# Hybrid encoder trunk on one core: HT as eight tiles that also hold the first adaLN weights, a division moved behind the weighted sums, gelu moved to where its results are loaded

## Chip, cores and metric

One core of one Trainium2 chip runs the whole kernel. The metric is the device time of one execution in microseconds (us), as the median of several runs. "Profile" means one execution taken by the hardware profiler. TensorE is named PE in its rows (PEld its weight loads), VectorE DVE, ScalarE ACT, GpSimd POOL, SyncE SP.

## What is computed

A two-layer encoder trunk on x of 1024 frames x 1024 channels, float32 in and out. Each layer runs a mixer and a feed-forward part, each behind an RMS norm with adaLN shift and scale and a gated residual:

```python
for layer in range(DEPTH):
    mod = cond @ ada_w[layer] + ada_b[layer]
    sh1, sc1, g1, sh2, sc2, g2 = jnp.split(mod, 6, axis=-1)
    h = modulate(rms_norm(x, ln_mix_g[layer]), sh1, sc1)
    ...
    x = x + g1[:, None, :] * mix
    h = modulate(rms_norm(x, ln_ffn_g[layer]), sh2, sc2)
    x = x + g2[:, None, :] * swiglu(h, ffn_w_in[layer], ffn_w_out[layer])
```

Layer 0 mixes with chunked softmax attention (8 heads of 64, clipped relative bias) beside an S5 scan, whose output goes through gelu and a gate; layer 1 with retention (4 heads of 128) beside stick-breaking attention. The two places of layer 0 that the change touches:

```python
p = jax.nn.softmax(s, axis=-1).astype(vb.dtype)
return jnp.einsum('bhqk,bkhd->bqhd', p, vb)
...
y = jax.nn.gelu(y.reshape(bsz, L, B_WIDTH))
gate = jax.nn.sigmoid(y @ w_glu.astype(f32) + b_glu.astype(f32))
return (y * gate).astype(u.dtype)
```

## The kernel before

**Dense products.** Every dense product keeps float32 accuracy by splitting each operand into a high part (rounded to fp32r) and a low part (the rest); `mm3` (L235) issues three matmuls, hi x hi, hi x lo, lo x hi, so rows of lines L237, L238 and L239 come in threes. The normed activations, transposed, are `HT` (L173): one tile of 128 partitions x 2 (hi, lo) x 8 (k) x 1024 frames. Streamed weights come through four `raw` buffers, and `Stream.split` (L125) makes hi and lo in one of six `whl` slots (128 x 2 x 1024) or, for the feed-forward output weights, of two `wo` slots: ScalarE copies hi (L130), GpSimd subtracts for lo (L131). The hidden activations of the feed-forward parts are `aT` (128 x 2 x 1024 each). A row mm<-HT,whl is a matmul into a bank "mm" whose streaming operand (named first) is a slice of HT or of whl, whichever the source code passes second; a row at<-aT,wo is the feed-forward output product.

**Where they lie.** In the built program, HT starts at byte 2,176 of each partition (hi of k at 2,176 + 4,096 k, lo 32,768 further on), whl slot j at 85,216 + 8,192 j, the aT tiles at 186,208 + 8,192 j, and the wo slots at 210,784 and 218,976. lo follows hi by 4,096 bytes in whl, wo and aT.

**Banks.** PSUM has three "mm" banks (L224), four "at" banks (L227) and one "av" bank (L230).

**Order.** The program is written as generators on a clock of ticks (`Pipe`, L42): `yield n` puts the rest of a step n ticks later, and each tick also pumps the weight stream. A feed-forward tick issues 24 large products. The tile layer then places the instructions on each engine; inside `high_priority` they go as early as they may.

**The opening** (`first`, L345). Eight x tiles are loaded and squared, `rms` (L303) turns the sums into 1/rms per frame: column sums on TensorE (L309), a power on GpSimd, a diagonal tile on VectorE (L319), and a product with ones that spreads it over the partitions (L325). The adaLN shift and scale of each k come from `cols(k)`: eight 32-row products of the silu'd condition with the ada0 weights (L370, into the av bank), a copy on ScalarE (L373), two one-column products (L376), and two additions on VectorE (L379, L381). ada0 weights pass through three rooms: two in U (a tile needed only later) and one of their own; the load of k + 3 is issued when k is done (L382). `scale(k)` multiplies x by 1/rms (L389), `turn(k)` applies shift and scale and writes hi (L396) and lo (L397) of HT's row k, and the first projection (wu) follows k by k in five banks. `s5_params` (L723) computes the scan's parameters in many VectorE steps of 16 elements; its first call stands behind n == 0 (L430).

**Attention** (`a_unit`, L581, 64 units: 8 heads x 8 tiles of queries). Scores on TensorE, bias and row minimum on VectorE (L590), Exp with row sums on ScalarE (L595), the reciprocal of the sums and a multiply of the 128 x (128 to 640) weights on VectorE (L597, L598), transposes (L503) and their copies, and products with v into the av bank; after four units of a head pair, hi is copied (L615) and lo subtracted (L616) into HT.

**Scan and gate.** `s5_block` (L916) ends each of its eight blocks with gelu out of PSUM on ScalarE (L974), then transposes (L985) and writes to DRAM; `glu` (L993) loads that twice, once through the weight stream (`yglu`, which gets hi and lo) and once as `yv`, for the last multiply. Rows ACT_TABLE_LOAD are ScalarE's loads of a function table; here they stand at L974 and at L595 (Exp).

**Norms behind a residual.** `norm` (L328) calls `rms` for 512 frames, then writes HT's rows through two "nf" buffers. Behind the first feed-forward part, four `v_tile` steps (L451) project v, and their copies `ve` (L460) out of PSUM also use "nf".

## Time and profile before

| | |
|---|---|
| Three runs | 2706.62, 2700.36, 2694.06 us; median 2700.36 us |
| Profiled execution | own time 2702.07 us, span of its records 2700.3 us |
| Mean granted TensorE clock | 0.982 |
| Instructions | 32542 |
| Busy: TensorE, its weight loads | 2591.9 us (96% of the span), 2115.7 us |
| Busy: VectorE, ScalarE, GpSimd | 1161.8, 709.3, 812.5 us |
| Moved by DMA | 267.11 MB |

The time of a run covers the span and a little around it (1.8 us in the profiled execution). TensorE's matmuls overlap: the next one starts before the last has ended, so "busy" is time in which at least one is under way, and the pace is read from start to start. The granted clock is a fraction of full speed, 2.4 GHz.

### The profile page before, as it was taken

The page shows a single profiled execution, that of the slowest core. Times are in us where ns is not written, and L with a number is a line of the kernel's source. Part 1 is how long each engine was busy: PE and PEld are TensorE (multiplying, and loading weights), DVE is VectorE, ACT ScalarE, POOL GpSimd, SP SyncE. Part 2 cuts the span into 40 slices and gives each one's busy share as a digit, 9 for nine tenths or more (in the row PEclk, how much of TensorE's full clock was granted, in tenths as well). Part 3 has the DMA queues.
Part 4 walks back from the last instruction along what each step waited for, and adds up shares of the span by engine and source line. Part 5 has one row for each costly group of instructions (what it writes and reads, how often), then busy time and mean ns, then how long its engine had stood idle before and what let it go on. Part 6 is the DMA issues. An engine that isn't in the chain of part 4 may idle for free. (4 is left out here: it accounts for less than half of the span.)

```text
span 2700.3 us, 32542 instructions
## 1 busy us (share of the span) xinstructions
PE 2591.9 (96%) x12880; PEld 2115.7 (78%) x12880; DVE 1161.8 (43%) x2164; ACT 709.3 (26%) x1287; POOL 812.5 (30%) x536
## 2 busy tenths in 40 slices
PE   5999898999999999999999999999999999999999
PEld 3898676777888888888778778787778888888887
DVE  7376675464333322222521466765632222222223
ACT  4332567322111111111221344444321111111100
POOL 4365103423322222222212133333232222222211
PEclk8999999999999999999999999999999999999999
DMA  7277764543233311111234332234311111111101
GB/s 274 82 227 226 191 188 150 180 140 109 86 110 109 109 48 47 47 47 47 78 94 152 91 100 86 62 95 152 109 63 47 47 47 47 47 47 47 48 16 63
DMA packets 145479, 267.11 MB, mean 99 GB/s; under 512 B 34416, under 2 KB 82224, under 8 KB 144560
## 3 DMA queue, kind: packets, MB, share of 16 engines
q1 hardware_dynamic: 145328, 265.05, 31.0%
q8 instruction: 101, 1.65, 0.3%
q14 instruction: 50, 0.41, 0.1%
HBM read 221.22 MB, written 45.88 MB: 99 GB/s over the span
## 5 line engine op out<-in xcount | busy, mean ns | idle before, releaser
L238 PE MATMUL mm<-HT,whl 128*128 128x512 f32 x1744 | 694.8, 399 | 2.6 <-DVE HT L340 2.5
L239 PE MATMUL mm<-HT,whl 128*128 128x512 f32 x1744 | 693.9, 398 | 0.0
L237 PE MATMUL mm<-HT,whl 128*128 128x512 f32 x1744 | 691.9, 398 | 0.2
L131 POOL TENSOR_TENSOR whl<-raw,whl 128x1024 fp32r<-128x1024 f32 x142 | 346.3, 2447 | 670.6 <-ACT whl L130 665.0
L238 PEld LDWEIGHTS mm<-HT,whl 128*128 128x128 f32 x1744 | 329.9, 189 | 85.0 <-DVE HT L340 5.1
L237 PEld LDWEIGHTS mm<-HT,whl 128*128 128x128 f32 x1744 | 329.5, 189 | 81.0 <-ACT HT L624 0.7
L239 PEld LDWEIGHTS mm<-HT,whl 128*128 128x128 f32 x1744 | 329.7, 189 | 80.0 <-issue 1.0
L1323 DVE SCALAR_TENSOR_TENSOR x<-at,col,x 128x512 f32<-128x512 f32 x352 | 262.7, 750 | 270.7 <-PE at L239 270.5
L1308 DVE TENSOR_TENSOR sg<-sg,mm 128x512 f32<-128x512 f32 x88 | 60.5, 688 | 666.2 <-PE mm L239 666.1
L239 PE MATMUL at<-aT,wo 128*128 128x512 f32 x704 | 275.5, 391 | 0.0
L237 PE MATMUL at<-aT,wo 128*128 128x512 f32 x704 | 275.4, 394 | 0.0
L238 PE MATMUL at<-aT,wo 128*128 128x512 f32 x704 | 275.3, 391 | 0.0
L237 PE MATMUL mm<-whl,HT 128*128 128x512 f32 (+1 forms) x688 | 252.3, 367 | 9.1 <-ACT ve L460 5.9
L238 PE MATMUL mm<-whl,HT 128*128 128x512 f32 (+1 forms) x688 | 248.2, 361 | 0.0
L239 PE MATMUL mm<-whl,HT 128*128 128x512 f32 (+1 forms) x688 | 245.7, 362 | 0.0
L131 POOL TENSOR_TENSOR wo<-raw,wo 128x1024 fp32r<-128x1024 f32 x44 | 105.4, 2416 | 442.6 <-ACT wo L130 442.5
L130 ACT CAST whl<-raw 128x1024 fp32r<-128x1024 f32 x154 | 161.0, 1053 | 193.0 <-PE mm L239 178.3
L1310 POOL TENSOR_TENSOR aT<-sg,aT 128x512 fp32r<-128x512 f32 x88 | 116.3, 1322 | 306.2 <-DVE aT L1309 298.3
L1307 ACT ACTIVATE sg<-mm 128x512 f32<-128x512 f32 x88 | 52.5, 597 | 540.8 <-PE mm L239 540.8
L130 ACT CAST wo<-raw 128x1024 fp32r<-128x1024 f32 x44 | 44.1, 1047 | 497.3 <-PE at L239 490.1
L237 PEld LDWEIGHTS mm<-whl,HT 128*128 128x128 f32 x688 | 138.6, 201 | 27.7 <-ACT ve L460 6.7
L237 PEld LDWEIGHTS at<-aT,wo 128*128 128x128 f32 x704 | 132.6, 188 | 29.8 <-issue 0.5
(290 smaller groups left out, 3221.7 us busy)
## 6 DMA issues: line engine op xcount, KB each, us to landing
raw<-in_ffn_w_in SPq DMA_DIRECT2D x88, 512.0 KB, 3.5
raw<-in_ada_w SPq DMA_DIRECT2D x80, 512.0 KB, 4.1
raw<-in_ffn_w_out SPq DMA_DIRECT2D x44, 512.0 KB, 3.3
qkd<-stk SPq DMA_DIRECT2D x32, 256.0 KB, 4.7
q<-qkd SPq DMA_DIRECT2D x64, 128.0 KB, 4.1
ks<-qkd SPq DMA_DIRECT2D x32, 256.0 KB, 4.4
qkd<-stk SPq DMA_DIRECT2D x16, 512.0 KB, 2.8
raw<-in_cd_w_in_c SPq DMA_DIRECT2D x16, 512.0 KB, 4.4
```

Of the source, the lines that this page charges most:

```text
L130: nc.scalar.copy(hi, u.raw[:, :u.n])
L131: self.low.tensor_sub(lo, u.raw[:, :u.n], hi.bitcast(F32))
L237: mm(out, lhs.hi, rhs.hi, start=start, stop=False)
L238: mm(out, lhs.hi, rhs.lo, start=False, stop=False)
L239: mm(out, lhs.lo, rhs.hi, start=False, stop=stop)
L1307: nc.scalar.activation(sg, gu[0], AF.Silu)
L1308: nc.vector.tensor_mul(sg, sg, gu[1])
L1310: nc.gpsimd.tensor_sub(a[m].lo[:, sl], sg, a[m].hi[:, sl].bitcast(F32))
L1323: nc.vector.scalar_tensor_tensor(xh, ps, self.col[layer, 5][:, n:n + 1], xh, M, A)
```

## The change

It has these parts:

1. **HT** becomes eight tiles, one for each k, of 128 x 2 x 1024, so that lo of a k follows hi by 4,096 bytes (`Rows` picks the tile). In the built program they start at 2,272 + 8,192 k; whl starts at 85,216 as before; aT at 186,272 and wo at 210,848.
2. **Opening.** The ada0 weights of k are loaded into the room of HT's tile k, all issued ahead, with one load of the weight stream behind every second k, so no load waits for a room. The columns of k + 1 and the products of k + 2 are started ahead of the first projection's products of k - 1, the low parts of streamed weights are made by VectorE instead of GpSimd in this stage, multiplies by 1/rms move into `turn`, and `params` is not called behind n == 0.
3. **Attention.** Reciprocal and multiply of the weights go (L597, L598). Row sums of four units of a head pair are collected in `rc` (128 x 4 x 2); behind the last, one reciprocal, a broadcast to 128 x 512 on GpSimd, four transposes into an "at" bank, a copy on ScalarE and a multiply with the av bank on VectorE, and then hi and lo.
4. **Gelu** leaves the scan's blocks: ScalarE copies there, and gelu runs on the streamed `yglu` tiles ahead of their split (4 of 1024 columns) and on `yv` (2 of 2048) in the gate.
5. **Norms.** `rms` waits two ticks instead of one between the sums and the diagonal tile, and `v_tile` behind the first feed-forward part takes its copies from the "hf" buffers instead of "nf".

The core of the diff (`PAD` was 0 and goes; the order of three small constants in the constructor changes too):

```diff
@@ Stream.split
+        if u.act is not None:
+            nc.scalar.activation(u.raw[:, :u.n], u.raw[:, :u.n], u.act)
         nc.scalar.copy(hi, u.raw[:, :u.n])
@@ Trunk.__init__
-        HT = self.const.tile([P, 2, NK, T], F32R, name="HT")
-        self.HT = Split(HT[:, 0], HT[:, 1])
+        self.ht = [self.const.tile([P, 2, T], F32, tag=f"HT{k}", name="ada0") for k in range(NK)]
+        self.HT = Split(Rows(self.ht, 0), Rows(self.ht, 1))
@@ rms
-        yield 1
+        yield 2
@@ first
+        ada0 = list(self.ht)
+
         def load(k):
             for q in range(2):
-                c0 = q * 1024
-                nc.sync.dma_start(out=slot(k)[:, c0:c0 + 1024], in_=I["ada0"][k, :, q * 1024:(q + 1) * 1024])
+                nc.sync.dma_start(out=ada0[k][:, q], in_=I["ada0"][k, :, q * 1024:(q + 1) * 1024])
...
-            if k + 3 < NK:
-                load(k + 3)
             yield
-        def scale(k):
+        def turn(k):
+            self.ht[k] = self.const.tile([P, 2, T], F32R, tag=f"HT{k}", name="HT")
             for half in range(2):
                 sl = slice(half * 512, half * 512 + 512)
                 v.tensor_mul(xs[:, k, sl], xs[:, k, sl], self.rb[half])
...
-        load(0)
-        self.stream.dma()
-        load(1)
-        load(2)
-        self.stream.dma()
+        for k in range(NK):
+            load(k)
+            if k % 2:
+                self.stream.dma()
...
+        self.stream.low = v
+        live = [cols(k) for k in range(NK)]
...
             if n < NK:
-                next(live[n])
-                scale(n)
                 turn(n)
                 if n + 1 < NK:
-                    live.append(cols(n + 1))
-                    next(live[-1])
-            if n == 0:
-                next(params)
+                    next(live[n + 1])
+                if n + 2 < NK:
+                    next(live[n + 2])
...
+        self.stream.low = nc.gpsimd
@@ a_unit
-        nc.scalar.activation(pw[:, :W], pw[:, :W], AF.Exp, bias=st[:, 0:1], scale=-1.0, accum_out=st[:, 2:3])
-        yield 1
-        nc.vector.reciprocal(st[:, 3:4], st[:, 2:3])
-        nc.vector.tensor_scalar(pw[:, :W], pw[:, :W], st[:, 3:4], None, M)
-        yield 1
+        if i % 4 == 0 and hd % 2 == 0:
+            self.rc = self.sm.tile([P, 4, 2], F32, tag="arc", bufs=2, name="arc")
+        rc = self.rc
+        nc.scalar.activation(pw[:, :W], pw[:, :W], AF.Exp, bias=st[:, 0:1], scale=-1.0, accum_out=rc[:, i % 4, hd % 2:hd % 2 + 1])
+        yield 2
...
+        if i % 4 == 3:
+            nc.vector.reciprocal(rc, rc)
+            f = pool.tile([P, 640], F32, tag="pw", bufs=5, name="af")[:, :512]
+            nc.gpsimd.tensor_copy(f.rearrange("p (a d) -> p a d", d=64),
+                                  rc.rearrange("p i u -> p (i u)").unsqueeze(2).to_broadcast([P, 8, 64]))
...
+        rb = self.at_bank()
+        for j in range(4):
+            nc.tensor.transpose(rb[:, j * P:j * P + P], f[:, j * P:j * P + P], self.ident)
...
-        nc.scalar.copy(hi, av)
-        nc.vector.tensor_sub(lo, av, hi.bitcast(F32))
+        nc.scalar.copy(f, rb)
+        nc.vector.tensor_mul(f, f, av)
+        nc.scalar.copy(hi, f)
+        nc.vector.tensor_sub(lo, f, hi.bitcast(F32))
@@ s5_block
-        nc.scalar.activation(yg[:, :, (b % 2) * 64:(b % 2) * 64 + 64].rearrange("p t (g h) -> p g t h", h=16),
-                             yb.rearrange("p (g t h) -> p g t h", g=4, t=8), AF.Gelu_apprx_tanh)
+        nc.scalar.copy(yg[:, :, (b % 2) * 64:(b % 2) * 64 + 64].rearrange("p t (g h) -> p g t h", h=16),
+                       yb.rearrange("p (g t h) -> p g t h", g=4, t=8))
...
-                c.units[0].ready = True
+                c.units[0].ready, c.units[0].act = True, AF.Gelu_apprx_tanh
@@ glu
+                if m == 0:
+                    nc.scalar.activation(yv[u], yv[u], AF.Gelu_apprx_tanh)
@@ the program behind ffn 0
-            pipe.tick(k.v_tile(xp, "nf", k.wdv, t))
+            pipe.tick(k.v_tile(xp, "hf", k.wdv, t))
```

In the changed program the lines are some 11 further on: `mm3` is L248 to L250, the diagonal product L336, the column additions L390 and L392, the low part in the stream L142.

How the built order of instructions moves, at three places.

TensorE where the first norm half behind a feed-forward part begins. Before, the sums (L309, four columns) and the product with the diagonal tile (L325, dgt) stand next to each other:

```order
L238 MATMUL mm<-HT,whl 128x512
L239 MATMUL mm<-HT,whl 128x512
L309 MATMUL at<-ones,acc 128x1 x4
L325 MATMUL at<-dgt,ones 128x512
L237 MATMUL at<-aT,wo 128x512
L238 MATMUL at<-aT,wo 128x512
L239 MATMUL at<-aT,wo 128x512
```

With the change (L320 and L336), first

```order
L250 MATMUL mm<-HT,whl 128x512
L320 MATMUL at<-ones,acc 128x1 x4
L248 MATMUL at<-aT,wo 128x512
L249 MATMUL at<-aT,wo 128x512
L250 MATMUL at<-aT,wo 128x512
```

and then, 24 such products behind the sums (the first two rows are the last of them),

```order
L249 MATMUL at<-aT,wo 128x512
L250 MATMUL at<-aT,wo 128x512
L336 MATMUL at<-dgt,ones 128x512
L248 MATMUL at<-aT,wo 128x512
L249 MATMUL at<-aT,wo 128x512
```

So the diagonal product has moved behind one tick's 24 output products.

VectorE in the opening, from the second k's column additions (L379) on. Before (ag is a small constant, L748 to L698 are the scan's parameters, xs the x tiles):

```order
L379 TENSOR_TENSOR col_108<-av,adab 128x1 x2
L389 TENSOR_TENSOR xs<-xs,at 128x512
L396 CAST HT<-tf 128x512
L389 TENSOR_TENSOR xs<-xs,at 128x512 x2
L262 TENSOR_SCALAR ag<-ag 128x1
L748 TENSOR_TENSOR ang<-s5par,dt 128x16
L381 SCALAR_TENSOR_TENSOR col_108<-col_108,lng 128x1
L691 TENSOR_SCALAR rn<-ang 128x16
L692 TENSOR_SCALAR rn<-rn 128x16
L693 TENSOR_SCALAR rn<-rn 128x16
L698 SCALAR_TENSOR_TENSOR ang<-rn,ang 128x16 x2
L396 CAST HT<-tf 128x512
```

The third k's additions stand 37 rows further on, after all the parameter steps of that call. With the change (L390 and L392 the additions), the first and second column additions:

```order
L390 TENSOR_TENSOR col_114<-av,adab 128x1 x2
L392 SCALAR_TENSOR_TENSOR col_114<-col_114,lng 128x1
L399 TENSOR_TENSOR xs<-xs,at 128x512 x8
L402 CAST HT<-tf 128x512
L399 TENSOR_TENSOR xs<-xs,at 128x512 x8
L390 TENSOR_TENSOR col_114<-av,adab 128x1 x2
```

and behind the third (L142 the low part of a weight unit, L765 to L715 the parameters, L390 the fourth addition):

```order
L273 TENSOR_SCALAR ag<-ag 128x1
L402 CAST HT<-tf 128x512
L781 TENSOR_TENSOR den<-s5par 128x16
L142 TENSOR_TENSOR whl<-raw,whl 128x1024
L765 TENSOR_TENSOR ang<-s5par,dt 128x16
L708 TENSOR_SCALAR rn<-ang 128x16
L709 TENSOR_SCALAR rn<-rn 128x16
L710 TENSOR_SCALAR rn<-rn 128x16
L715 SCALAR_TENSOR_TENSOR ang<-rn,ang 128x16
L142 TENSOR_TENSOR whl<-raw,whl 128x1024
L715 SCALAR_TENSOR_TENSOR ang<-rn,ang 128x16
L390 TENSOR_TENSOR col_114<-av,adab 128x1 x2
```

So the additions of the first three k stand ahead of every parameter step, and some of these steps stand between the third and the fourth, with low parts among them.

ScalarE behind the first feed-forward part (L339 writes hi of HT from nf, L300 squares, L460 copies ve). Before:

```order
L339 ACTIVATE HT<-nf,col_6688 128x512 x2
L300 ACTIVATE hf<-x_5101 128x512
L300 ACTIVATE hf<-x_5102 128x512
L300 ACTIVATE hf<-x_5103 128x512
L300 ACTIVATE hf<-x_5104 128x512
L339 ACTIVATE HT<-nf,col_6688 128x512 x4
L460 COPY ve<-mm 128x512
L339 ACTIVATE HT<-nf,col_6688 128x512 x3
L460 COPY ve<-mm 128x512
L339 ACTIVATE HT<-nf,col_6688 128x512
L460 COPY ve<-mm 128x512 x2
```

With the change (L350, L311, L467):

```order
L350 ACTIVATE HT<-nf,col_6668 128x512 x2
L311 ACTIVATE hf<-x_5083 128x512
L311 ACTIVATE hf<-x_5084 128x512
L350 ACTIVATE HT<-nf,col_6668 128x512 x4
L467 COPY ve<-mm 128x512 x2
L350 ACTIVATE HT<-nf,col_6668 128x512 x2
L467 COPY ve<-mm 128x512
L350 ACTIVATE HT<-nf,col_6668 128x512 x2
L467 COPY ve<-mm 128x512
L350 ACTIVATE HT<-nf,col_6668 128x512 x4
```

So the first copies of ve have moved from the middle of the second half's eight L339 rows to ahead of them.

## Rows read from the trace of the kernel before

**Rows 1.** The page's first part: busy time, share of the span, instructions.

```profile
PE 2591.9 (96%) x12880; PEld 2115.7 (78%) x12880; DVE 1161.8 (43%) x2164; ACT 709.3 (26%) x1287; POOL 812.5 (30%) x536
```

**Rows 2.** Stretches: length, busy us of PE, PEld, DVE, ACT, POOL, clock, DMA, GB/s.

```profile
0.00:25.00 25.00, 7.67 (x48) 5.49 (x52) 10.41 (x24) 12.01 (x19) 5.14 (x11) 1.00 0.90 343
25.00:50.00 25.00, 10.63 (x50) 6.09 (x42) 22.54 (x49) 9.87 (x13) 22.56 (x12) 0.79 0.76 290
50.00:75.00 25.00, 23.04 (x121) 19.65 (x122) 21.19 (x121) 7.33 (x12) 7.69 (x6) 0.86 0.33 106
280.00:480.00 200.00, 175.69 (x1317) 137.60 (x1316) 131.71 (x495) 137.22 (x293) 29.57 (x22) 0.97 0.62 173
2000.00:2690.00 690.00, 690.00 (x2974) 559.20 (x2973) 171.84 (x251) 84.47 (x99) 190.90 (x99) 1.00 0.14 45
```

**Rows 3.** TensorE's groups by shape: count, busy us, mean ns, idle before, releaser.

```profile
L238 PE MATMUL mm<-HT,whl 128*128 128x512 f32 x1744 | 694.8, 399 | 2.6 <-DVE HT L340 2.5
L238 PE MATMUL at<-aT,wo 128*128 128x512 f32 x704 | 275.3, 391 | 0.0
L238 PE MATMUL mm<-whl,HT 128*128 128x512 f32 x432 | 175.3, 406 | 0.0
```

**Rows 4.** Timeline of TensorE at changes of product: start us, length us, instruction.

```profile
2302.35 0.40 PE L237 MATMUL at<-aT,wo 128*128 128x512 f32 x1
...
2307.83 0.40 PE L239 MATMUL mm<-HT,whl 128*128 128x512 f32 x1
...
2321.11 0.40 PE L237 MATMUL mm<-HT,whl 128*128 128x512 f32 x1
...
2362.57 0.39 PE L237 MATMUL at<-aT,wo 128*128 128x512 f32 x1
...
1388.22 0.40 PE L237 MATMUL mm<-whl,HT 128*128 128x512 f32 x1
...
1410.62 0.39 PE L237 MATMUL mm<-HT,whl 128*128 128x512 f32 x1
```

**Rows 5.** Waits of TensorE: line, releaser, us in total, times, longest us.

```profile
PE av L370 <- issue: 15.4, 2, 9.3
PE at L325 <- DVE dgt L319: 7.0, 3, 4.4
PE mm L237 <- ACT ve L460: 5.9, 1, 5.9
PE at L557 <- DVE qk L551: 5.6, 3, 4.1
PE at L985 <- ACT yg L974: 4.1, 3, 2.4
```

**Rows 6.** Timeline of the opening, idle time before and its releaser in brackets.

```profile
38.94 3.56 DVE L698 SCALAR_TENSOR_TENSOR ang<-rn,ang 128x16 f32<-128x16 f32 x2
...
50.71 0.22 DVE L379 TENSOR_TENSOR col<-av,adab 128x1 f32<-128x1 f32 x2
...
51.02 1.93 PE L370 MATMUL av<-U,scz 128*32 128x256 f32 x16 [9.26 <-issue]
```

**Rows 7.** Stretches behind the two stalls after the first feed-forward part.

```profile
1330.00:1335.00 5.00, 5.00 (x14) 3.31 (x13) 3.29 (x5) 1.39 (x2) 0.53 (x1) 0.67 0.27 98
1370.00:1375.00 5.00, 5.00 (x15) 3.94 (x14) 4.23 (x6) 2.51 (x5) 0.00 (x0) 0.57 0.15 38
```

**Rows 8.** Groups of VectorE and ScalarE from 280 to 480 us.

```profile
L598 DVE TENSOR_SCALAR pw<-pw,ast 128x640 f32<-128x640 f32 (+4 forms) x64 | 32.6, 513 | 0.9
...
L974 ACT ACT_TABLE_LOAD x8 | 10.3, 1283 | 0.1
...
L597 DVE RECIPROCAL ast<-ast 128x1 f32<-128x1 f32 x64 | 10.1, 157 | 18.5 <-ACT pw L595 18.4
```

**Rows 9.** Timeline of TensorE at four transposes and the product behind them.

```profile
186.59 0.60 PE L557 MATMUL at<-ident,qk 128*128 128x128 f32 x4
186.95 0.36 PE L237 MATMUL mm<-whl,HT 128*128 128x256 f32 x1
```

More of the change, by code (lines that the diff above doesn't have):

```diff
@@ L25 @@
 FB = 2
-PAD = 0
 EPS = 1e-6
@@ L39, in __getitem__, with __init__ @@
         return Split(self.hi[ix], self.lo[ix])
+class Rows:
+    def __init__(self, tiles, part):
+        self.tiles, self.part = tiles, part
+    def __getitem__(self, ix):
+        return self.tiles[ix[1]][ix[0], self.part, ix[2]]
 class Pipe:
@@ L74, in __init__ @@
         self.raw = self.w = self.freed = self.issued = None
-        self.ready = True
+        self.ready, self.act = True, None
 class Chunk:
@@ L127, in split @@
         u = self.units[self.ns]
-        hl = self.pool[u.tag].tile([P, 2, 1024 + PAD], F32R, tag=u.tag, bufs=self.cap[u.tag], name=u.tag)
+        hl = self.pool[u.tag].tile([P, 2, 1024], F32R, tag=u.tag, bufs=self.cap[u.tag], name=u.tag)
         hi, lo = hl[:, 0, :u.n], hl[:, 1, :u.n]
+        if u.act is not None:
+            nc.scalar.activation(u.raw[:, :u.n], u.raw[:, :u.n], u.act)
         nc.scalar.copy(hi, u.raw[:, :u.n])
@@ L172, in __init__ @@
         nc.vector.memset(self.ones, 1.0)
-        HT = self.const.tile([P, 2, NK, T], F32R, name="HT")
-        self.HT = Split(HT[:, 0], HT[:, 1])
+        self.r8 = self.const.tile([P, 16], F32, name="r8")
+        self.mhalf = self.const.tile([P, 1], F32, name="mhalf")
+        nc.vector.memset(self.mhalf, -0.5)
+        self.ht = [self.const.tile([P, 2, T], F32, tag=f"HT{k}", name="ada0") for k in range(NK)]
+        self.HT = Split(Rows(self.ht, 0), Rows(self.ht, 1))
         for name, shape in (("mixd", [NK, P, T]), ("cad", [P, 16, 2, P]), ("m2d", [P, 16, 2, P]), ("ed", [P, 16, 2, P]),
@@ L178, in __init__ @@
             setattr(self, name, self.dr.tile(shape, F32, name=name))
-        self.r8 = self.const.tile([P, 16], F32, name="r8")
-        self.mhalf = self.const.tile([P, 1], F32, name="mhalf")
-        nc.vector.memset(self.mhalf, -0.5)
         self.col, self.acc, self.state, self.pp = {}, {}, None, None
@@ L351, in first @@
         uf = U.rearrange("p g s h -> p (g s h)")
-        ax = xp.tile([P, 2048], F32, name="ax")
-        slot = lambda k: ax if k % 3 == 2 else uf[:, k % 3 * 2048:k % 3 * 2048 + 2048]
         cs = self.const.tile([P, 2, NK], F32, name="col0")
@@ L369, in cols @@
                 r = i % 4 * 32
-                nc.tensor.matmul(ps[r:r + 32, :256], scz[:, i], slot(k)[:, i * 256:i * 256 + 256], start=i < 4, stop=i > 3)
+                nc.tensor.matmul(ps[r:r + 32, :256], scz[:, i], ada0[k][:, i // 4, i % 4 * 256:i % 4 * 256 + 256],
+                                 start=i < 4, stop=i > 3)
             row = xp.tile([P, 256], F32, tag="row", bufs=2, name="row")
@@ L389, in scale @@
                 v.tensor_mul(xs[:, k, sl], xs[:, k, sl], self.rb[half])
-        def turn(k):
-            for half in range(2):
-                sl = slice(half * 512, half * 512 + 512)
                 f = xp.tile([P, 512], F32, tag="tf", bufs=3, name="tf")
@@ L416, in first @@
                 v.tensor_add(ac[:, sl], ac[:, sl], sq)
-        for _ in self.rms(xp, ac):
-            pass
-        pipe.tick()
-        live = [cols(0)]
+        self.stream.low = v
+        live = [cols(k) for k in range(NK)]
+        r = self.rms(xp, ac)
+        next(r)
         next(live[0])
+        next(r)
+        next(live[0])
+        next(r, None)
+        next(live[1])
         for n in range(NK + 1):
             if n < NK:
-                next(live[n])
-                scale(n)
                 turn(n)
                 if n + 1 < NK:
-                    live.append(cols(n + 1))
-                    next(live[-1])
-            if n == 0:
-                next(params)
+                    next(live[n + 1])
+                if n + 2 < NK:
+                    next(live[n + 2])
             if n > 0:
```

## Prediction

> **What bounds the kernel.** I read the page's busy times first: TensorE is busy for 2591.9 us of the 2700.3 us span [rows 1], so a change gains only by taking away TensorE's idle 108 us or by making its matmuls follow each other faster. The table of stretches says where the idle time lies. From 0 to 75 us TensorE works for 41.3 of 75 us; beside attention (280 to 480) it is idle for 24 us; in the second feed-forward part (2000 to 2690) it is busy without a gap, at a granted clock of 1.00, the 2.4 GHz level [rows 2]. Most of the time is therefore matmul pace. The table of matmul groups and then the timeline give it. One 128x512 product mm<-HT,whl lasts 399 ns, one at<-aT,wo 391 ns [rows 3], but they overlap; what counts is start to start. In the second feed-forward part, 24 products at<-aT,wo run from 2302.35 to 2307.83, which is 5.48 us or 228.3 ns each, and 177 products mm<-HT,whl from 2321.11 to 2362.57, 41.46 us or 234.2 ns each [rows 4]. Same width, same type, no wait, full clock, 13 us apart: 5.9 ns differ. With the operands exchanged, 96 products mm<-whl,HT take 1388.22 to 1410.62, 233.3 ns each [rows 4].
>
> What separates the two kinds is where their operands lie. aT and wo tiles start at distances that are multiples of 8,192 bytes, and every slice of them is a multiple of 512 bytes further on, so moving and stationary operand always lie a multiple of 512 bytes apart. HT begins at byte 2,176 and the whl slots at 85,216 + 8,192 j: 96 bytes off such a multiple, for every k, slot and half.
>
> **A. The pace of the products with HT.** The change puts the eight HT tiles at 2,272 + 8,192 k, hi and lo 4,096 apart, so that all their distances to whl are multiples of 512; aT and wo keep theirs. If distance sets the pace, HT products go at the 228.3 ns of aT. Forward products: 3 x 1,744 = 5,232 [rows 3], times 234.2 - 228.3 = 5.9 ns, is 30.9 us. Exchanged ones: 3 x 432 = 1,296 [rows 3] at 5 ns; 768 of them (four heads, eight tiles, 24 each) belong to the retention stage, where TensorE also waits for others, and I count those half: 528 x 5 + 768 x 2.5 = 4.6 us. The 3 x 256 products of 256 columns have no twin at a 512-byte distance; between nothing and half of 5.9 ns each (2.3 us) I take 1. Together 30.9 + 4.6 + 1, or -36 us; bounds 0 (distance is not the cause) and -40 (all of it on the path).
>
> Against this speaks a rule of the Trainium skill, "TensorE: Matmul & The Clock Gate", section "Step-by-step: what each phase is for": TensorE reads the streaming operand and the weights through two independent SBUF ports, so loading the next weights takes no bandwidth from the running matmul. By that rule distance would change nothing and A would be 0. The trace has two paces for one instruction in one stretch [rows 4], which the rule doesn't explain, so I go by the rows.
>
> **B. The opening.** Before, TensorE waits 15.4 us for the adaLN products at L370 [rows 5], 9.3 of it before 51.02 [rows 6]. The weights are not what is late: that product needs the single av bank, which is free only once VectorE has added the previous columns (L379, at 50.71) [rows 6]. VectorE stood in the scan's parameter steps; two of them, 16 elements wide, took 3.56 us from 38.94 [rows 6], while GpSimd, busy for 22.56 of 25 us [rows 2], made low halves. The change gives those low halves to VectorE, lets the column products run one k ahead, and no longer starts the parameter steps after the first k. All sixteen ada0 pieces are issued at once: 4.2 MB of x, 8.4 of ada0 and 2.1 of weights at 343 GB/s [rows 2] have landed by about 43 us, so transfers aren't the limit. But the order of VectorE shows parameter steps still standing between the additions of the third k and the fourth, and later, and six low halves in the same queue (0.8 us each by the 0.51 us of a multiply of up to 640 columns [rows 8], an estimate, about 5 us). Bounds: -24 (the 15.4 us, and the clock at 0.79 and 0.86 over 25 us each, 8.7 us [rows 2]) and +5 (stall stays, low halves come on top). I take -7, the stall halved, near the upper end, because the chain from additions over ScalarE, VectorE and GpSimd to the product is as long as before.
>
> **C. Attention and GLU.** The change drops 64 multiplies of the weights and 64 reciprocals, 32.6 and 10.1 us of VectorE [rows 8]; VectorE has 68 of 200 us to spare there [rows 2], so that pays only where TensorE waits for it. Activation tables: gelu's 8 loads of 1.283 us [rows 8] and Exp's 10 become 10 in all, since gelu no longer alternates with Exp; TensorE's wait for gelu, 4.1 us, goes [rows 5]. Added: 8 x 4 transposes at 0.09 us (four stand from 186.59 to 186.95 [rows 9]), 3 us of TensorE; eight copies, broadcasts and multiplies off TensorE, covered while ScalarE and VectorE keep their 63 and 68 us of 200 [rows 2]; and gelu before the first GLU product, a table load and two 1,024-wide steps, about 3 us ahead of TensorE. -4 + 3 + 3 = +2 us; bounds -10 and +20 (rival 3).
>
> **D. The norms.** TensorE waits 7.0 us in all at L325, 4.4 of it once, for the diagonal tile [rows 5]: L325 stands directly behind the sums it depends on. One more tick puts a tick's 24 products, 24 x 0.2283 = 5.5 us, between them, longer than the wait. Behind the first feed-forward part it waits 5.9 us for ve [rows 5], a copy that queues behind the second half's norm on ScalarE because it shares the nf buffers; in the change's order two of these copies stand ahead of that half. After each stall the clock is at 0.67 and 0.57 (at 1.2 GHz for part of it) for 5 us more [rows 7], 1.7 + 2.1 us. Saved: 4.4 + 5.9 + 3.8 = 14 us. The same tick makes HT late, up to 5.5 us at its first reader; I take 4. -10 us; bounds -14 and 0.
>
> **Sum.** -36 - 7 + 2 - 10 = -51 us, against the profiled execution's own 2702.07 us: 2651 us. That execution lies 1.7 us above the median of the three runs, less than they differ among themselves, and I leave it there. A measurement of this kernel can tell about 0.5%, 13.5 us, from no change.
>
> **Rivals.**
> 1. *The pace isn't the distance's.* Then A is 0 and 2651 + 36 = 2687 us remains. For it: the rule above, and aT and HT differ in more than place (who writes them, how often one is read). Against it: the paces stand in the same stretch with all engines at work, and switch within one product. Chance 0.09.
> 2. *The scan's set-up comes due all at once* (slower). VectorE did 43.7 us of work between 25 and 75 us [rows 2]. If the shorter opening pushes that into the projections behind it, where TensorE already waits 5.6 us for VectorE at L557 [rows 5], and the first scan block needs its result, TensorE waits for up to 43.7 us, and the 9.3 us stall remains too: 2651 + 7 + 53 = 2711 us. It decides above a loss of about 51 us. Against it: VectorE's order still starts these steps within the opening. Chance 0.03.
> 3. *Dividing late holds the bank.* There is one av bank; it now waits for a broadcast, four transposes, a copy and a multiply after its last product, where one copy and one subtraction stood. If 2.5 us of that are uncovered in each of eight groups, C is +22 and the time 2671 us. Chance 0.12.
> 4. *The opening gains all of it*: B at -24, 2634 us. Chance 0.10.
>
> **How the numbers follow.** The forecast, 2651 us, keeps 0.66; within it A between -40 and -27 and D between -14 and -5 give 2643 to 2665. The range 2630 to 2685 takes in rivals 3 and 4 and leaves out rival 2 and most of rival 1. Faster by over 0.5% means below 2687: forecast, rivals 3 and 4 and half of rival 1, 0.92. Within 0.5%: the other half, 0.05. Slower: 0.03.
>
> **What would show it.** A: in the second feed-forward part 177 products mm<-HT,whl in about 40.4 us (228.3 ns), the 399 ns of one down to about 391; at 41.4 us A is wrong. B: the copies out of the first projection's banks some 7 us earlier; L370's successor waiting for VectorE at 50 us would mean no gain. C: no table load on the scan's copies, VectorE 40 us less busy beside attention, and a wait at the av products if rival 3 holds. D: no wait at the successors of L325 and of ve behind the first feed-forward part, and a short new one at HT. If the total falls and the 177 products still take 41.4 us, the sum was right for the wrong reason.

## The result

The changed kernel takes 2633.78 us (median; 2628.13 to 2636.47), the kernel before 2703.49 beside it: ratio 0.9744, 95% interval 0.9711 to 0.9778, some 70 us less. Forecast were 2651 us in a range from 2630 to 2685. Its profiled execution took 2628.13 us, with a span of 2626.3 and a mean clock of 0.992 (before 0.982); it is the fastest of the four.

Page of the changed kernel, first part (answers to [rows 1]):

```profile
PE 2535.4 (97%) x12912; PEld 2104.9 (80%) x12912; DVE 1134.9 (43%) x2058; ACT 708.9 (27%) x1293; POOL 809.5 (31%) x538
```

TensorE's busy time fell by 56.5 us, its idle time from 108.4 to 90.9. So most of the gain is time in which TensorE works (its matmuls follow each other faster), and part of it is waiting.

Stretches of the changed kernel, columns as in [rows 2]; attention lies 11 us earlier, so its 200 us begin at 268, and the short stretch at 1300 holds the product with the diagonal tile behind the first feed-forward part (before: the first row of [rows 7]):

```profile
0.00:25.00 25.00, 7.68 (x37) 5.38 (x38) 11.13 (x22) 11.91 (x19) 2.84 (x10) 1.00 0.90 345
25.00:50.00 25.00, 20.57 (x106) 14.74 (x105) 18.62 (x40) 12.27 (x17) 12.44 (x9) 0.93 0.89 343
50.00:75.00 25.00, 19.76 (x126) 15.64 (x125) 24.54 (x133) 9.19 (x16) 11.68 (x8) 1.00 0.16 52
268.00:468.00 200.00, 177.25 (x1352) 141.61 (x1351) 105.82 (x384) 138.32 (x300) 35.03 (x30) 0.97 0.62 173
1300.00:1305.00 5.00, 4.00 (x16) 2.96 (x17) 3.23 (x5) 1.89 (x3) 0.95 (x1) 1.00 0.64 238
1960.00:2622.00 662.00, 662.00 (x2913) 546.45 (x2912) 174.27 (x253) 79.15 (x93) 181.31 (x95) 1.00 0.14 47
```

From 25 to 50 us TensorE now works for 20.57 us in place of 10.63, at 0.93 instead of 0.79. Behind the norm the clock stays at 1.00, where it was 0.67.

Groups by shape (answer to [rows 3]):

```profile
L249 PE MATMUL mm<-HT,whl 128*128 128x512 f32 x1744 | 680.3, 390 | 4.5 <-DVE HT L351 4.4
...
L249 PE MATMUL at<-aT,wo 128*128 128x512 f32 x704 | 274.9, 390 | 1.9 <-POOL aT L1329 1.9
...
L249 PE MATMUL mm<-whl,HT 128*128 128x512 f32 x432 | 171.8, 398 | 0.0
```

All three kinds now last 390 to 398 ns. Timeline of TensorE where one kind of product gives way to another (answer to [rows 4]):

```profile
2189.24 0.39 PE L248 MATMUL mm<-HT,whl 128*128 128x512 f32 x1
...
2229.41 0.39 PE L248 MATMUL at<-aT,wo 128*128 128x512 f32 x1
...
2236.01 0.39 PE L248 MATMUL at<-aT,wo 128*128 128x512 f32 x1
...
2241.48 0.39 PE L250 MATMUL mm<-HT,whl 128*128 128x512 f32 x1
...
1344.38 0.39 PE L248 MATMUL mm<-whl,HT 128*128 128x512 f32 x1
...
1366.14 0.39 PE L248 MATMUL mm<-HT,whl 128*128 128x512 f32 x1
```

The 177 products mm<-HT,whl take 2189.24 to 2229.41, 226.9 ns each (before 234.2); 24 products at<-aT,wo 227.9 (before 228.3); 96 exchanged ones from 1344.38 to 1366.14 226.7 (before 233.3).

Waits of TensorE: line, releaser, us in total, times, longest (answers to [rows 5]):

```profile
PE mm L248 <- ACT HT L402: 8.1, 6, 2.8
...
PE mm L249 <- DVE HT L351: 4.4, 6, 1.4
...
PE av L380 <- issue: 2.5, 4, 1.0
...
PE mm L248 <- ACT HT L350: 1.5, 3, 0.7
...
PE at L1002 <- ACT yg L991: 0.6, 1, 0.6
...
PE av L521 <- DVE af L631: 0.6, 2, 0.4
...
PE mm L248 <- ACT ve L467: 0.3, 1, 0.3
...
PE at L336 <- DVE dgt L330: 0.2, 1, 0.2
```

The 15.4 us at the adaLN products are 2.5, the 7.0 at the diagonal product 0.2, the 5.9 for ve 0.3, the 4.1 for gelu 0.6. New are 8.1 us at HT in the opening (2.8 before) and 4.4 + 1.5 at HT behind the norms (2.5 before at the first of these).

To see where 74 us of span went, both executions are cut at the starts of the same instructions. The last column is the run a1 below, in which only the place of HT differs from before. One execution of each is cut.

| stage, us | before | changed | HT's place alone |
|---|---|---|---|
| 1 to the last product of the first projection's fifth bank | 95.7 | 84.7 | 96.2 |
| 2 to attention's first scores | 183.4 | 183.3 | 184.6 |
| 3 attention, to the output projection | 200.7 | 197.4 | 200.7 |
| 4 to the first at<-aT,wo | 179.8 | 177.6 | 173.7 |
| 5 to the first sums of the norm | 664.5 | 651.4 | 650.1 |
| 6 to the second half's sums | 34.6 | 24.5 | 35.3 |
| 7 to layer 1's first scores | 147.4 | 139.7 | 143.1 |
| 8 to the sums in layer 1's second norm | 426.6 | 421.3 | 424.5 |
| 9 to the first at<-aT,wo there | 95.5 | 87.6 | 92.7 |
| 10 to the last product's end | 668.3 | 655.1 | 653.8 |
| sum | 2696.5 | 2622.6 | 2654.7 |

HT's place gives 41.8 of the 73.9 us. Of the other 32.1, stage 1 holds 11.5, stages 6, 7 and 9 (the norms) 10.8 + 3.4 + 5.1 = 19.3, attention 3.3; the rest is small and of both signs. Stage 4 is 3.9 us longer. It begins where the gate's last products end, and c2 below, which differs from the changed kernel only in gelu's place, takes 173.0 us there, against 175.9 or more in every run with gelu in the gate. That points to the gelu in the gate, though not to how it costs TensorE time.

Two cautions. By the medians, each beside its own kernel before, the whole change gives 70 us and HT's place 42, which leaves 28: the execution of a1 cut here is the slowest of its four, that of the changed kernel the fastest, so 32.1 is some 4 us too much. And stages that no edit touches differ from run to run. Attention takes 195.3 to 204.0 us in the runs with the changed kernel's code there, and stage 1 takes 84.7 to 88.2 in the nine with its opening. Stage 9 takes 87.6 us in a4, b1, c2 and d2 as it does in the changed kernel, but 92.3 in b2 and a3 and 90.8 in b3, where the granted clock falls behind the first sums. Here is that stretch in b2, columns as in [rows 2]; in the changed kernel the clock stays at 1.00 there:

```profile
1901.00:1906.00 5.00, 5.00 (x17) 4.32 (x18) 0.17 (x1) 0.00 (x0) 0.00 (x0) 0.50 0.02 3
```

### The profile page after: what moved, and what is told of

The parts are those of the page before. It is cut to its first block, busy times and chain, and to the rows that moved or that the text cites. A ratio compares the mean times of both kernels' runs of the same rounds, so it can differ in the third digit from the quotient of the medians.

```text
span 2626.3 us, 32531 instructions
## 1 busy us (share of the span) xinstructions
PE 2535.4 (97%) x12912; PEld 2104.9 (80%) x12912; DVE 1134.9 (43%) x2058; ACT 708.9 (27%) x1293; POOL 809.5 (31%) x538
## 5 line engine op out<-in xcount | busy, mean ns | idle before, releaser
L249 PE MATMUL mm<-HT,whl 128*128 128x512 f32 x1744 | 680.3, 390 | 4.5 <-DVE HT L351 4.4
L248 PE MATMUL mm<-HT,whl 128*128 128x512 f32 x1744 | 680.7, 391 | 1.8 <-ACT HT L350 1.5
L250 PE MATMUL mm<-HT,whl 128*128 128x512 f32 x1744 | 679.8, 390 | 0.0
L142 POOL TENSOR_TENSOR whl<-raw,whl 128x1024 fp32r<-128x1024 f32 x136 | 332.5, 2453 | 494.5 <-ACT whl L141 487.8
L248 PEld LDWEIGHTS mm<-HT,whl 128*128 128x128 f32 x1744 | 327.7, 188 | 72.8 <-ACT HT L350 2.8
L250 PEld LDWEIGHTS mm<-HT,whl 128*128 128x128 f32 x1744 | 327.9, 188 | 68.5
L250 PE MATMUL at<-aT,wo 128*128 128x512 f32 x704 | 274.8, 390 | 0.0
L248 PE MATMUL at<-aT,wo 128*128 128x512 f32 x704 | 273.1, 391 | 0.0
L248 PE MATMUL mm<-whl,HT 128*128 128x512 f32 (+1 forms) x688 | 249.5, 363 | 8.6 <-ACT HT L402 8.1
L249 PE MATMUL mm<-whl,HT 128*128 128x512 f32 (+1 forms) x688 | 244.8, 356 | 0.0
L142 POOL TENSOR_TENSOR wo<-raw,wo 128x1024 fp32r<-128x1024 f32 x44 | 107.4, 2464 | 442.4 <-ACT wo L141 442.4
L250 PE MATMUL mm<-whl,HT 128*128 128x512 f32 (+1 forms) x688 | 242.1, 357 | 0.0
L248 PEld LDWEIGHTS mm<-whl,HT 128*128 128x128 f32 x688 | 138.0, 201 | 25.7 <-ACT HT L402 10.7
```

The costliest lines, as they stand in the source:

```text
L142: self.low.tensor_sub(lo, u.raw[:, :u.n], hi.bitcast(F32))
L248: mm(out, lhs.hi, rhs.hi, start=start, stop=False)
L249: mm(out, lhs.hi, rhs.lo, start=False, stop=False)
L250: mm(out, lhs.lo, rhs.hi, start=False, stop=stop)
```

## The experiments

Times are medians beside the kernel before on the same chip; a row without an interval has one time. The kernel before has a median of 2696.8 to 2705.1 us beside the different runs, so where a few us matter the ratios are the safer comparison. 177 products mm<-HT,whl of the second feed-forward part stand for the pace.

| run | us | ratio to before, interval | ns per mm<-HT,whl |
|---|---|---|---|
| changed kernel | 2633.78 | 0.9744 [0.9711, 0.9778] | 226.9 |
| a1 before, HT 96 bytes further on | 2657.24 | 0.9843 [0.9814, 0.9871] | 226.7 |
| a2 changed, HT 96 bytes back | 2679.86 | 0.9927 [0.9900, 0.9955] | 234.3 |
| a4 changed, off by 256 | 2630.28 | one time | 226.9 |
| e1 changed, off by 64; aT by 128, 32 | 2665.13 | one time | 229.0 |
| a3 changed, aT and wo mixed | 2651.70 | one time | 227 |
| b1 changed, old opening | 2646.80 | 0.9813 [0.9786, 0.9840] | |
| b2 changed, low parts on GpSimd | 2650.17 | 0.9805 [0.9775, 0.9835] | |
| b3 old opening, low parts on VectorE | 2642.89 | 0.9805 [0.9781, 0.9828] | |
| c1 changed, weights divided | 2636.90 | 0.9755 [0.9730, 0.9779] | |
| c2 changed, gelu in the scan | 2630.51 | 0.9736 [0.9713, 0.9759] | |
| d1 changed, one tick in the norm | 2640.92 | 0.9776 [0.9751, 0.9800] | |
| d2 changed, ve in nf | 2648.13 | 0.9796 [0.9767, 0.9826] | |

### Is it the distance? (a1, a2)

a1, the kernel before with one statement moved:

```diff
+        self.r8 = self.const.tile([P, 16], F32, name="r8")
+        self.mhalf = self.const.tile([P, 1], F32, name="mhalf")
         HT = self.const.tile([P, 2, NK, T], F32R, name="HT")
...
-        self.r8 = self.const.tile([P, 16], F32, name="r8")
-        self.mhalf = self.const.tile([P, 1], F32, name="mhalf")
```

> The kernel before with two small constants (96 bytes of a partition) allocated ahead of HT instead of behind it, and nothing else: HT starts at byte 2,272 in place of 2,176, whl stays at 85,216, so that all distances between the two become multiples of 512 bytes, with HT still one tile. If the distance sets the pace: products mm<-HT,whl go from 234.1 ns to the 227.2 ns seen with the change, start to start, which for 5,232 of them is 36 us, and with the exchanged ones (1,296 at some 5 ns) and fewer stretches at a low clock 36 to 45 us in all: 2659 to 2668 us beside 2704 before, ratio about 0.985. If the pace came from HT being eight tiles, or from any other part of the change: 234 ns stay, ratio 1.000 within 0.003.

a2 moves the same lines in the changed kernel the other way, behind the eight tiles:

```diff
-        self.r8 = self.const.tile([P, 16], F32, name="r8")
-        self.mhalf = self.const.tile([P, 1], F32, name="mhalf")
         self.ht = [self.const.tile([P, 2, T], F32, tag=f"HT{k}", name="ada0") for k in range(NK)]
...
+        self.r8 = self.const.tile([P, 16], F32, name="r8")
+        self.mhalf = self.const.tile([P, 1], F32, name="mhalf")
```

> The changed kernel with the same two constants put back behind HT: HT's eight tiles start at 2,176 + 8,192 k, whl at 85,216, 96 bytes off a multiple of 512 again. If the distance sets the pace: 234 ns for mm<-HT,whl, and 36 to 45 us slower than the changed kernel (2670 to 2679 us, ratio to before about 0.989). If not: the changed kernel's 2634 us, ratio 0.974.

Timeline of a1, the first and the next product after 177 of mm<-HT,whl:

```profile
2287.55 0.39 PE L237 MATMUL mm<-HT,whl 128*128 128x512 f32 x1
...
2327.68 0.39 PE L237 MATMUL at<-aT,wo 128*128 128x512 f32 x1
```

and of a2:

```profile
2302.98 0.39 PE L248 MATMUL mm<-HT,whl 128*128 128x512 f32 x1
...
2344.44 0.39 PE L248 MATMUL at<-aT,wo 128*128 128x512 f32 x1
```

40.13 us against 41.46: 226.7 and 234.3 ns. With nothing but 96 bytes moved, the kernel before loses 42 us, and the changed one gains back 46. One tile or eight, the opening, the norms play no part in the pace. The distance theory stands; rival 1 falls.

### Which distances? (a3, a4, e1)

a3 pads the aT tiles and the wo slots:

```diff
-                aT = fp.tile([P, 2, T], F32R, tag="aT", bufs=FB + 1, name="aT")
+                aT = fp.tile([P, 2 * T + (16, 16, 96)[m % 3]], F32R, tag=f"aT{m % 3}", name="aT")
...
+            hl = self.pool[u.tag].tile([P, 2048 + 64 * (1 - j)], F32R, tag=f"wo{j}", name=u.tag)
```

> The changed kernel with pads of 64 to 384 bytes between the three aT tiles and the two wo slots of the feed-forward parts, so that the distance between aT and wo takes six values modulo 512: 0, 64, 128, 256, 320 and 384; HT and whl stay at multiples of 512. If only multiples of 512 are good: products at 0 keep 227 to 232 ns start to start, those at the other five take about 234 ns, so five sixths of 2,112 products cost some 10 us. If a smaller power of two is enough (256, 128 or 64), the groups at its multiples keep 227 ns as well. If distance plays no part for aT and wo: all six groups alike.

It did not tell the groups apart: by distance, the means from start to start were 232.8 ns at 0, 231.4 at 64, 231.4 at 128, 232.3 at 256, 233.6 at 320 and 231.5 at 384. These are distances to the weights of the product behind; by the distance to a product's own weights the means (of steps under 250 ns) are 232.3, 231.6, 231.0, 232.8, 233.4 and 232.2, no clearer. Even the pairs at a good distance were slow. In this loop the distance changes every three products, so each good pair stands next to bad ones; that one product's delay carries over to the next would explain it, but is not shown. So I read only stretches of one distance, which a4 and e1 make.

a4 allocates four more constants (256 bytes) ahead of HT, and uses them where they were allocated before:

```diff
+        self.ct = self.const.tile([P, NK], F32, name="ct")
+        self.sc = self.const.tile([P, NK], F32, name="scond")
+        self.lng = self.const.tile([P, 2, 2, NK], F32, name="lng")
+        self.cs0 = self.const.tile([P, 2, NK], F32, name="col0")
         self.r8 = self.const.tile([P, 16], F32, name="r8")
```

> The changed kernel with four more constants (256 bytes) ahead of HT, so that every distance between HT and whl is 256 bytes off a multiple of 512, the same for all products. If 512 is the step that counts: 234 ns for mm<-HT,whl and some 45 us more, about 2675 to 2680 us. If a step of 256, 128 or 64 is enough: 227 ns and the changed kernel's time, about 2630 to 2636 us.

```profile
2256.88 0.39 PE L252 MATMUL mm<-HT,whl 128*128 128x512 f32 x1
...
2297.04 0.39 PE L252 MATMUL at<-aT,wo 128*128 128x512 f32 x1
```

This timeline of a4 gives 40.16 us for 177: 226.9 ns. A step of 256 is enough.

e1 moves only col0 (64 bytes) ahead of HT, and puts a gap between aT and wo:

```diff
                 a[m] = Split(aT[:, 0], aT[:, 1])
+                if m == 0:
+                    fp.tile([P, 8 if layer else 32], F32, name="gap")
```

> The changed kernel with three uniform shifts: HT 64 bytes off a multiple of 512 from whl, everywhere; aT off by 128 bytes from wo in the first feed-forward part and by 32 in the second. Shifted by 96 the HT products took 234 ns, by 256 they took 227. If 256 is the step that counts: 234 ns in all three. If 128: the aT products of the first part keep 227 to 229 ns, HT and the second part's aT go to 234. If 64: HT and the first part's aT keep 227 to 229, only the second part's aT go to 234. The second part's aT are slow in every case, since 96 is a multiple of 32.

Timeline of e1: 177 products mm<-HT,whl, then 24 at<-aT,wo of the first feed-forward part, then 24 of the second, each with the product behind them:

```profile
2286.57 0.39 PE L249 MATMUL mm<-HT,whl 128*128 128x512 f32 x1
...
2327.11 0.39 PE L249 MATMUL at<-aT,wo 128*128 128x512 f32 x1
...
1128.18 0.40 PE L249 MATMUL at<-aT,wo 128*128 128x512 f32 x1
...
1133.78 0.39 PE L251 MATMUL mm<-HT,whl 128*128 128x512 f32 x1
...
2148.19 0.40 PE L249 MATMUL at<-aT,wo 128*128 128x512 f32 x1
...
2153.80 0.39 PE L249 MATMUL mm<-HT,whl 128*128 128x512 f32 x1
```

229.0 ns for HT at 64, 233.3 for aT at 128 and 233.8 for aT at 32 (the groups of either part lie between 232 and 234). None of my three cases holds as written: 128 is as bad as 32, so of the steps tried below 512 only 256 costs nothing, but 64 costs only 2 ns as long as HT streams. With HT as weights (448 off) it is some 233 ns. The run also settles whose place counts. In a1 and a2 HT moved, the streaming operand, and the weights stayed; here aT stays where it was and wo, the weights, lies behind the gap. Either changes the pace, so it isn't the place of one operand alone.

### The opening (b1, b2, b3)

b1 puts the old `first` into the changed kernel (ada0 in three rooms, one column product ahead, low parts on GpSimd). Its core:

```diff
-        self.stream.low = v
-        live = [cols(k) for k in range(NK)]
+        live = [cols(0)]
...
+            if n == 0:
+                next(params)
...
-        self.stream.low = nc.gpsimd
```

> The changed kernel with the opening of before (ada0 through three rooms in U and its own, one column product ahead, low parts on GpSimd, parameter steps started behind the first k); HT stays eight tiles at the new place. If the 11 us by which the first projection ends earlier (84.7 us, before 95.7) are the new opening's own: the end goes back to 94 to 96 us and the whole time to about 2645 us, ratio 0.978. If they come from HT's place or tiles: the end stays near 85 us and the time at 2634, ratio 0.974. The 9 us stall before the third k's adaLN products is back in the first case.

The first projection's fifth bank ends at 97.2 us, the run is 13 us longer (19 by the ratios), and the wait at the adaLN products is back, 17.5 us in all: the 11 us are the new opening's own, and none of them HT's place (96.2 in a1). Which part of it? b2 leaves out the two lines that move the low parts to VectorE:

```diff
-        self.stream.low = v
...
-        self.stream.low = nc.gpsimd
```

> The changed kernel with the low parts of streamed weights left on GpSimd in the opening (VectorE loses 6.7 us of work between 33 and 85 us, GpSimd, busy for 29 of these 52 us, takes some 12 us more). If moving them to VectorE is part of the 11 us won: the first projection ends at 87 us or later (84.7 in the changed kernel), and the time rises by 2 to 8 us. If the gain is that of the order (columns ahead, parameter steps later) and VectorE is now the tight engine: the end is at 85 us or earlier, and the time the same or up to 3 us less.

The end is at 93.5 us: without that move 8.8 of the 11 us are lost. The whole run is 16 us longer, where I expected 2 to 8; the rest lies in stages with the changed kernel's code, stage 9 above all (4.7 us). Timeline of b2, GpSimd and VectorE from 47 us on, and TensorE behind them:

```profile
47.96 2.39 POOL L142 TENSOR_TENSOR whl<-raw,whl 128x1024 fp32r<-128x1024 f32 x1
...
48.06 2.32 DVE L706 TENSOR_SCALAR rn<-ang 128x16 f32<-128x16 f32 x1
...
51.72 4.63 POOL L142 TENSOR_TENSOR whl<-raw,whl 128x1024 fp32r<-128x1024 f32 x2
...
51.85 4.53 DVE L713 SCALAR_TENSOR_TENSOR ang<-rn,ang 128x16 f32<-128x16 f32 x2
...
57.11 1.93 PE L380 MATMUL av<-ada,scz 128*32 128x256 f32 x16 [6.38 <-issue]
```

A VectorE step of 16 elements lasts 2.32 us and two more 4.53, each until the GpSimd operation beside it ends; the adaLN product behind them waits 6.38 us. That the low parts come too late for their own products is not it: TensorE shows no wait for whl in the opening of b2. In the changed kernel the same steps are short, until one meets GpSimd:

```profile
49.24 0.23 DVE L709 TENSOR_SCALAR rn<-rn 128x16 f32<-128x16 f32 x1
...
53.16 2.55 POOL L403 TENSOR_TENSOR HT<-tf,HT 128x512 fp32r<-128x512 f32 x2 [1.04 <-DVE rz L721]
...
53.19 1.29 DVE L730 TENSOR_SCALAR sn<-rz 128x16 f32<-128x16 f32 x1
```

Between 20 and 100 us, 13 of 109 such steps take over 0.5 us in b2, 19.4 us together; before 10 (14.6 us), in the changed kernel 9 (11.2 us), in b3 7 (8.8 us). Every one of these 39 ends within 0.3 us of a GpSimd operation's end; the median step takes 0.17. The Trainium skill says so, "SBUF — State Buffer", section "SBUF: two separate sides": VectorE and GpSimd share a pair of ports, and where a VectorE instruction needs it (two operands in SBUF, or a two-port mode), whichever engine starts first holds it for its whole instruction while the other waits. The trace agrees for the 39 long steps.

b3 is the reverse, b1's old opening with just these two lines:

```diff
+        self.stream.low = v
         live = [cols(0)]
...
+        self.stream.low = nc.gpsimd
```

> The changed kernel with the opening of before, as in the run that ended its first projection at 97.2 us, but with the low parts of streamed weights on VectorE in it. There, VectorE's parameter steps of 16 elements, 0.17 us each as a rule, last 1.2 to 2.4 us where a GpSimd operation is under way, and end when it ends (10 of 109 steps, 13.6 us). If holding VectorE up is what the low parts on GpSimd cost: the first projection ends at 86 to 91 us and the whole time is 6 to 11 us below the 2647 us of that run (ratio 0.977 to 0.979). If the order is what counts, columns ahead and parameter steps later, and low parts only add to VectorE's queue: 95 us or later, 2645 us or more.

The end is at 88.8 us, 8.4 earlier than in b1. Over the whole run the gain (2642.89 against 2646.80, ratios 0.9805 and 0.9813) is not told apart from nothing. In the trace the old order keeps one long wait of TensorE:

```profile
PE mm L248 <- DVE HT L407: 6.0, 1, 6.0
```

So of the 11 to 12 us some 8 to 9 are the low parts' change of engine, and the rest the order; both are differences of single executions, and stage 1 varies by 3.5 us among runs with the same opening.

### Attention and gelu (c1, c2)

c1 has the attention unit of before:

```diff
-        yield 2
+        yield 1
+        nc.vector.reciprocal(st[:, 3:4], st[:, 2:3])
+        nc.vector.tensor_scalar(pw[:, :W], pw[:, :W], st[:, 3:4], None, M)
+        yield 1
...
-        nc.scalar.copy(f, rb)
-        nc.vector.tensor_mul(f, f, av)
-        nc.scalar.copy(hi, f)
-        nc.vector.tensor_sub(lo, f, hi.bitcast(F32))
+        nc.scalar.copy(hi, av)
+        nc.vector.tensor_sub(lo, av, hi.bitcast(F32))
```

> The changed kernel with the attention unit of before: reciprocal and multiply of the weights on VectorE are back, the four transposes, the broadcast and the late multiply go; gelu stays where the change put it. In the changed kernel the stretch from the first scores to the output projection takes 197.4 us, before 200.7. If, as the prediction has it, the late division itself brings nothing (TensorE does not wait for VectorE there, and 32 transposes come on top): 194 to 197 us, the whole time the same as the changed kernel's or up to 3 us less (ratio 0.973 to 0.975). If the 43 us less of VectorE is what shortens the stretch: 200 us or more, 3 us or more slower (ratio 0.976).

c2 has gelu at the end of the scan's blocks, as before (L974 there), and none at the loads:

```diff
-                c.units[0].ready, c.units[0].act = True, AF.Gelu_apprx_tanh
+                c.units[0].ready = True
...
-                if m == 0:
-                    nc.scalar.activation(yv[u], yv[u], AF.Gelu_apprx_tanh)
```

> The changed kernel with gelu back at the end of the scan's blocks (8 more table loads of 1.28 us on ScalarE) and none in the gate. By the prediction: TensorE's wait of 4.1 us for gelu comes back and 3 us of wait in the gate go, so the stretch from the first scores to the output projection stays within 2 us of 197.4. If the 3.3 us by which this stretch became shorter are due to gelu: 200 us or more, ratio 0.976.

Attention's stretch in the changed kernel, in c1 and in c2, one row of each:

```profile
268.00:465.40 197.40, 174.65 (x1327) 139.56 (x1325) 105.82 (x384) 135.72 (x295) 32.43 (x29) 0.97 0.63 176
```

```profile
269.10:473.20 204.10, 177.46 (x1322) 138.48 (x1320) 132.70 (x497) 135.19 (x291) 30.00 (x22) 0.97 0.62 171
```

```profile
270.50:472.10 201.60, 180.82 (x1348) 144.46 (x1347) 106.61 (x384) 138.68 (x298) 32.47 (x29) 0.95 0.62 173
```

197.4, 204.1 and 201.6 us, by which both runs fall into their second case and both parts would be worth some us. But the runs whose code in this stretch is the changed kernel's spread from 195.3 (a4) to 204.0 (a3), and the whole times of c1 and c2, 2636.90 and 2630.51, are within 4 us of the changed kernel's on either side. What either part is worth is below what these runs can tell. VectorE has 27 us less to do (105.82 against 132.70), and the end doesn't notice.

### The norms (d1, d2)

```diff
-        yield 2
+        yield 1
         rb = []
```

> The changed kernel with one tick instead of two between the sums and the diagonal tile of the norms. By the prediction: the waits at the product with the diagonal tile come back (7.0 us in all before, 4.4 of it behind the first feed-forward part), with some 2 us of low clock behind the longest, and the wait at HT (5.9 us in the changed kernel, L351 and L350 together) goes or shrinks: 3 to 7 us slower in sum (ratio 0.976). If the two ticks only shift the wait from one place to another: within 2 us of the changed kernel.

Waits of TensorE in d1, at the diagonal product and at the sums of the norms:

```profile
PE at L336 <- DVE dgt L330: 6.3, 3, 4.5
PE at L320 <- DVE acc L312: 5.0, 3, 2.3
```

and the stretches behind the first feed-forward part and in layer 1's second norm, columns as in [rows 2]:

```profile
1303.00:1308.00 5.00, 4.67 (x11) 3.09 (x12) 2.70 (x5) 1.38 (x2) 1.40 (x1) 0.60 0.31 105
...
1920.00:1925.00 5.00, 4.71 (x13) 3.81 (x14) 0.40 (x2) 1.88 (x2) 1.01 (x1) 0.52 0.31 105
```

6.3 us at the diagonal product again (0.2 with two ticks): 4.5 of it behind the first feed-forward part, where the clock behind it is 0.60, and 1.6 in layer 0's second norm. In layer 1 the diagonal product doesn't wait, neither here nor before the change; there TensorE waits 1.9 us for the second half's sums, and the clock of 0.52 stands behind that wait. Stages 6, 7 and 9 add up to 33.7 + 134.2 + 93.2 = 261.1 us, 9.3 more than in the changed kernel, 5.6 of them in stage 9, which varies as said above; the whole run is 7 us longer. The wait behind DVE HT falls from 4.4 to 3.2 us. d2 takes ve from nf:

```diff
-            pipe.tick(k.v_tile(xp, "hf", k.wdv, t))
+            pipe.tick(k.v_tile(xp, "nf", k.wdv, t))
```

> The changed kernel with the four copies ve back in the nf buffers of the norm. By the prediction: TensorE waits some 6 us for ve again behind the first feed-forward part, and runs at a low clock for 5 us behind it (2 us): the stretch from the second half's sums to layer 1's first scores grows from 139.7 us to about 146 to 148, and the whole time by 6 to 8 us, ratio 0.977. If the second tick of the norms, which gives the copies more room, is enough by itself: no wait, ratio 0.974.

The wait for ve in d2:

```profile
PE mm L248 <- ACT ve L467: 5.8, 2, 5.6
```

and the stretch from it on:

```profile
1345.00:1350.00 5.00, 4.55 (x11) 3.59 (x12) 1.14 (x2) 2.14 (x4) 0.00 (x0) 0.50 0.50 108
```

5.8 us of wait, and 5 us at a clock of 0.50 (1.2 GHz). Stage 7 grows from 139.7 to 147.8, as expected, and the whole run by 14 us, where I expected 6 to 8; the rest is spread over stages with the changed kernel's code. Both parts are needed, and behind the first feed-forward part each pays twice: once in the wait, once in the clock behind it.

## Why the prediction held, and where it didn't

**A, forecast -36.** Right in its cause, 6 us short in its size. HT's place alone is worth 42 us (a1). The mis-sized term is the pace at a good distance: I took the 228.3 ns of aT, measured were 226.9, which over 5,232 products is 7 us more. The 228.3 came from a group of 24 between slow HT products; in a1, where only HT moved, such groups take 227.1. By the rule of the Trainium skill that I weighed against it ("TensorE: Matmul & The Clock Gate", "Step-by-step: what each phase is for"), A would be 0; the runs a1 and a2 decide against it. I spoke of multiples of 512; the runs show that 256 serves too. The products of 256 columns, for which I took 1 us, gained nothing: 121.7 ns before, 121.5 now.

**B, forecast -7.** Measured -11 (stage 1; -7.5 to -11 over the nine runs with this opening). The stall at L370 is not halved but nearly gone (15.4 us to 2.5), and 5.3 us of waits at HT came in. The step that failed is the sentence that put the low parts into VectorE's queue as a cost of about 5 us. By b2 and b3 their move is most of the gain, since it keeps VectorE's small steps from waiting for GpSimd. The row was there: two steps of 16 elements in 3.56 us [rows 6], beside a GpSimd that was busy for 22.56 of 25 us [rows 2]. I read the one as a slow step and the other as a full queue, and didn't ask whether the first was long because of the second.

**C, forecast +2.** The sign isn't shown; attention's stretch is 3.3 us shorter, within the spread of 9 us. That VectorE's 43 us would not come off the end was right (its busy time beside attention fell by 27 us, not by the 40 I named). The 3 us for gelu in the gate fit c2, whose stage 4 is 4.7 us shorter without it. Rival 3, the late division holding the av bank, is out: TensorE waits 0.6 us there.

**D, forecast -10.** Measured -14 in stages 6 and 7, and up to -5 in stage 9; +7 and +14 when undone. The three terms behind the first feed-forward part came as written. Left out was layer 1's second norm, where TensorE waited 1.8 us for the second half's sums before the change, with the clock at 0.61 over 5 us behind it. Stage 9 is 5.1 us shorter than with HT's place alone, but b2, b3 and a3 have the two ticks and take 90.8 to 92.3 us there, so how much of that is the second tick's isn't shown. The late HT, 4 us in the sum, shows as 5.9 us of waits, 2.5 before.

**The total.** In the profiled execution the terms were short by 6, 4, 5 and up to 9 us, all on the same side, but that execution is 6 us below the median, and some of this is its luck; the measured 2634 us is 17 below the forecast, near the lower end of the range (2630). It is also the time that rival 4 gave, by another way: that rival had the opening gain 24 us and the rest as forecast. The opening gained 11. Without the stages, the agreement with rival 4 would have been taken for its proof. Rival 2 didn't come: TensorE's wait at the successor of L557 is 6.8 us, before 5.6.

## What to carry to other kernels

Where a kernel is bound by back-to-back matmuls, measure their pace start to start for each pair of operands, and where two kinds differ, look at the byte distance of the streaming operand from the weights: here, whole stretches at a multiple of 256 bytes went at 227 ns and most others at 233 to 234, and a few constants allocated in another order were worth 1.6%. On a VectorE chain, look at what GpSimd does beside small steps that last ten times their usual time: here each of them ended with a GpSimd operation, and taking work from GpSimd can free VectorE even when VectorE has to do that work itself. A wait of TensorE of some 5 us cost itself and some us of half clock behind it here, so what removes one pays twice. And before a few us of a stage are put down to an edit, see how far that stage varies in runs that don't touch it.

## What was not expected of the hardware

The pace of 128x512 products by distance modulo 512, in stretches of one distance: 226.9 ns at 0 and at 256, 229.0 at 64, 233.3 at 384 (aT, first part), 233.8 at 480 (aT, second part), 234.3 at 416; the last three are too close to be put in order. It doesn't follow the powers of two, since 64 is better than 384, and what makes it was not found. Where HT is the weights operand and the products have 256 columns, the offset of e1 (448) was even faster, 115.4 ns against 121.5 in the changed kernel (48 products from 131.01 to 136.55, and from 128.41 to 134.24). No version that uses this was tried.
